# Attention as a side pipeline: two steps per pair of blocks, values together with new scores and both transposes together, let in at half as many places

## The chip, the core and the metric

The kernel runs on one core of a Trainium2 chip. The metric is the device time of one execution in microseconds. The input is one sequence of 512 tokens with 1024 channels, all in float32.

## What is computed

The reference is one layer with two sublayers. The parts that matter here, cut from it:

```python
proj = x @ w_in                                   # q, k, v of 12 heads; zb; qc
# A: three groups of 4 heads, dilations 1, 4, 16, causal windows, 128-query blocks
s = einsum(qb, kb) * ATTN_SCALE + bias            # masked
p = exp(s - s.max(-1)); den = p.sum(-1)
o = einsum(p, vb) / den                           # groups combined by their softmax denominators
# B: gated spatial mixing of gelu(zb).  C: 4 heads of cross-attention into 256 memory tokens
gates = sigmoid(x @ w_gate + b_gate)              # one per branch and channel
merged = gates0 * (oa @ w_proj_a) + gates1 * (ob @ w_proj_b) + gates2 * (oc @ w_proj_c)
h = layer_norm(ALPHA * x + merged @ w_out)
out = layer_norm(ALPHA * h + conv_ffn(h))         # gated MLP with a causal width-3 convolution
```

## The kernel before

Every large product is done in three matmuls (`mm3`, line 220): each operand is split into a high part in the float32r form and the rest, and high x rest, rest x high and high x high are added in PSUM. ScalarE makes the high part of a weight (line 133), VectorE the rest (line 134). Weights stream in on SP's queue, two loads ahead, and are split two units ahead of their use. TensorE does the main work in this order: q and k, v, the two halves of zb (`zb_part`, called twice), mem transposed (`tm`), qc, kc and vc, 24 gate columns (`gate`, with the branch projections between them), the output projection, and the gated MLP.

Attention is side work. It is written as a Python generator, `side()`, and each call of `fill()` in the main work lets one step of it in, up to the next `yield`. First come the windowed heads (`attn_A`) and their combination, which fall into the zb, qc, kc and vc stages; then, from the flag `mix` on, the spatial gating and the cross-attention (`attn_C`), which fall into the gate stage. `fill()` stands after each of 16 row blocks in each half of zb, at some places of qc, kc and vc, and after every second k of the gates.

A `Pair` is two query blocks of one head. An item of the pipeline is two such pairs, of two neighbouring heads, with four pieces of work:
- scores (`sc`, matmuls at line 524). A head has 64 channels, so its matmul uses 64 rows of the array, and the two heads in turn use the two halves of the rows (`alternate`). For the undilated heads and for the cross-attention a block has three matmuls (`mm3_ops`); for the dilated heads it has two in plain float32, which the trace shows as two instructions each.
- softmax on VectorE (bias and maximum, line 475) and ScalarE (exp, line 480), then the division on VectorE.
- transposes (`pt`, line 493): the full array, four or three matmuls of 128 columns per pair, and a copy by ScalarE from PSUM to `pT` (lines 495 to 498).
- values (`oT`, also line 524): the output has 64 rows, so the heads use the two halves of the array's columns.

In the pipeline before, an item takes four steps: scores of item i; the transposes of the first head of item i-1; those of its second head; the values of item i-2. The windowed attention has 8 items, the cross-attention 4. The `sc`, `pt` and `oT` tiles share eight PSUM banks with the main work's accumulators, of which zb holds four.

The text of the kernel is not the order of the engines. The framework's scheduler takes the instructions in the order of the text and moves them by its own model of when each can start; the engines then run that fixed order, each strictly in its own sequence. Table loads of ScalarE, which it needs to change between exp, log and gelu/tanh, are put in afterwards, wherever the order asks for one.

Of the kernel before, what the change touches and what calls it, by code (L numbers as in the profile page):

```python
# [47 lines left out]


def bucket_rows():  # L50
    """Per dilation group the bucket (one-hot, rows 0-31) and the mask (row 32) of each diagonal."""
    rows = np.zeros((N_BUCKETS + 1, 3, VW), np.float32)
    for i in range(VW):
        for g in range(3):
            n = 255 - i if g == 0 else 127 - i
            if g == 0:
                ok, dist = 0 <= n <= 128, n
            elif g == 1:
                ok, dist = n >= 0, 4 * n
            else:  # L60
                ok, dist = n >= 0 and n % 4 == 0, 4 * n
            if ok:
                rows[int(bucket_of(np.array([dist]))[0]), g, i] = 1.0
            else:
                rows[N_BUCKETS, g, i] = NEG
    return rows
# [3 lines left out]
def layer_kernel(  # L70
# [10 lines left out]
    small = ctx.enter_context(tc.tile_pool(name="small", bufs=4))  # L81
# [9 lines left out]
    def bank(name):  # L91
        return psum.tile([P, 512], F32, tag="bank", name=name)

    # ---------------------------------------------------------------- weight stream
    loads, prepared = [], {}
    state = {"load": 0, "split": 0}
    units = []

    def add_load(shape, src, parts):
        """One DMA of `shape`; parts: function raw -> list of (hi shape, raw view)."""  # L100
        n = len(loads)
        loads.append((shape, src))
        for f in parts:
            units.append((n, f))
# [48 lines left out]
        add_load([P, 8, 256], src, [lambda r: r[:, :, 0:128], lambda r: r[:, :, 128:256]])  # L153

    def kcols(w, k0, nk, c0, nc_):
        """Rows k0*128.., a [128, nk, nc_] load in units of 1024 per partition."""
        src = w[k0 * P:(k0 + nk) * P, c0:c0 + nc_].rearrange("(k p) c -> p k c", p=P)
        per = 1024 // nc_
        parts = [lambda r, s=s: r[:, s:s + per, :] for s in range(0, nk, per)]
        add_load([P, nk, nc_], src, parts)  # L160
# [36 lines left out]
    LAST = 6  # L197
# [3 lines left out]
    for i in range(0, NF, 2):  # L201
        src_a = wup[:, i * P:i * P + 256].rearrange("(k p) c -> p k c", p=P)
        src_b = wup[:, D_FF + i * P:D_FF + i * P + 256].rearrange("(k p) c -> p k c", p=P)
        n = len(loads)
# [7 lines left out]
        krows(wdn, k, k < NF - LAST)  # L212

    def mm3_ops(ps, w, v, first, last):
        """ps += w.T @ v for operands split into (hi, lo)."""
        return ((ps, w[1], v[0], first, False), (ps, w[0], v[1], False, False), (ps, w[0], v[0], False, last))

    def mm3(*args):
# [7 lines left out]
        else:  # L226
            nc.vector.scalar_tensor_tensor(lo, src, scale, hi.bitcast(F32), op0=ALU.mult, op1=ALU.subtract)

    # ---------------------------------------------------------------- x, transposed and split
    xraw = []  # L230
    for h in range(2):
        xraw.append(T8(f"x{h}").rearrange("p (b a) c -> p b (a c)", b=2))
# [35 lines left out]
        v = [t[k // 4][:, k % 4, :].rearrange("p (l r) -> p r l", r=4)[:, r, :] for t in (xTh, xTl)]  # L268
        return v[0], v[1]

    # ---------------------------------------------------------------- small parameters
    rows = const.tile([P, P], F32, name="rows")
    nc.vector.memset(rows, 0.0)
    nc.gpsimd.dma_start(rows[0:66, :], conv_w[0].rearrange("c (t p) -> (c t) p", p=P))
# [56 lines left out]
                                    ps.rearrange("p (g q) -> p g q", g=4),  # L331
                                    maskT[:, None, :].to_broadcast([P, 4, P]), op=ALU.mult)

    # ---------------------------------------------------------------- q, k, v
    qk12 = [T8(f"qk{i}") for i in range(2)]
    qk0 = [T8(f"qk0{i}", F32R) for i in range(2)]

# [51 lines left out]
    for j in range(2, 12):  # L389
        w = unit()  # L390
        ps = bank("qk")
# [10 lines left out]
    for hb in range(2):  # L402
        ps = bank("v0")
        for bb in range(2):
            b = 2 * hb + bb
# [13 lines left out]
    for r in range(4):  # L419
        nc.scalar.activation(v12[:, r, :], pss[r], AF.Copy)  # L420

    # ---------------------------------------------------------------- attention pieces
    NM = const.tile([P, 48], F32, name="NM")
    DEN = const.tile([P, 48], F32, name="DEN")
    RD = const.tile([P, 48], F32, name="RD")

    class Pair:
        """Two query blocks of one head: scores, softmax, weighted values (transposed)."""

        def __init__(self, part, h, pr):  # L430
            self.part, self.h, self.pr = part, h, pr
# [3 lines left out]
            return P if self.part == 0 and self.pr == 0 and u == 0 else 0  # L435

        def score_ops(self):
            """Matmul arguments of the scores, in order."""
            part, h, pr = self.part, self.h, self.pr
            rp = slice((h % 2) * HD, (h % 2) * HD + HD)  # L440
            sc = bank("sc").rearrange("p (u c) -> p u c", u=2)
            self.sc = sc
            ops = []
            for u in range(2):
                b = 2 * pr + u
                bs = slice(b * P, (b + 1) * P)
                if part == 1:
                    for g in range(2):
                        j = 2 * (g + 1) + h // 2
                        ops.append((sc[:, u, g * P:(g + 1) * P], qkT(j)[rp, bs], qkT(6 + j)[rp, bs], True, True))  # L450
                elif part == 0:
                    lo = self.lo(u)
                    ops.extend(mm3_ops(sc[:, u, lo:256], [t[rp, bs] for t in qk0s(h // 2)],
                                       [t[rp, (b - 1) * P + lo:(b + 1) * P] for t in qk0s(6 + h // 2)], True, True))
                else:
                    ops.extend(mm3_ops(sc[:, u, :], [t[rp, h // 2, bs] for t in qcT],
                                       [t[rp, h // 2, :] for t in kcT], True, True))
            return ops
# [59 lines left out]
            return ops  # L518

    def alternate(a, b):  # L520
        """The matmuls of two heads in turn: they use different rows or columns of the array."""
        for pair in zip(a, b):
            for ps, w, v, first, last in pair:
                nc.tensor.matmul(ps, w, v, start=first, stop=last)  # L524

    def pipeline(groups):
        """groups: (part, first head, done); scores run two steps ahead of values."""
        items = [[Pair(part, h + i, pr) for i in range(2)] + [gi] for gi, (part, h, _) in enumerate(groups)
                 for pr in range(2)]
        dsts = {}  # L530
        n = len(items)
        for i in range(n + 2):
            if i < n:
                two = items[i][:2]
                alternate(*[it.score_ops() for it in two])
                for it in two:
                    it.softmax()
                yield
            if 0 <= i - 1 < n:
                for it in items[i - 1][:2]:  # L540
                    it.turn()
                    yield
            if i >= 2:
                a, b, gi = items[i - 2]
                if gi not in dsts:
                    dsts[gi] = bank("oT")
                alternate(a.value_ops(dsts[gi]), b.value_ops(dsts[gi]))
                if a.pr == 1:
                    groups[gi][2](dsts[gi])
                yield  # L550

    oA = T8("oA")
# [68 lines left out]
    def fill(n=1):  # L621
        for _ in range(n):
            next(gen, None)
# [2 lines left out]
        while flag not in ready:  # L626
            next(gen)

    # ---------------------------------------------------------------- gated spatial inputs, memory
    sgb = T8("sgb")  # L630
    nc.sync.dma_start(sgb[:, 0, :], sg_ln_g[0:1, :].to_broadcast([P, SG_W]))
    nc.sync.dma_start(sgb[:, 1, :], sg_ln_b[0:1, :].to_broadcast([P, SG_W]))
# [1 line left out]
    def zb_part(dst):  # L634
        pss = [bank(f"zb{b}") for b in range(NB)]
        for u in range(4):
            w = unit()
            for b in range(NB):
                for k2 in range(2):
                    k = 2 * u + k2  # L640
                    xh, xl = xs(k, slice(b * P, (b + 1) * P))
                    mm3(pss[b], (xh, xl), (w[0][:, k2, :], w[1][:, k2, :]), k == 0, k == KD - 1)
                fill()
        for b in range(NB):
            nc.scalar.activation(dst[:, b, :], pss[b], AF.Gelu_apprx_tanh)

# [56 lines left out]
    for b in range(2):  # L703
        for k in range(KD):
            w = ws_[k // 4]
            bs = slice(b * P, (b + 1) * P)
            mm3(ps[:, b * 256:b * 256 + 256], (mTh_[:, k, bs], mTl_[:, k, bs]),
                (w[0][:, k % 4, :], w[1][:, k % 4, :]), k == 0, k == KD - 1)
            if k % 4 == 3:
                fill()  # L710
    nc.vector.tensor_copy(vcN, ps.rearrange("p (b c) -> p b c", b=2))
    ready.add("mix")

    # ---------------------------------------------------------------- spatial gating, cross-attention
    obT_h = T8("obTh", F32R)
    obT_l = T8("obTl", F32R)
    ocT = T8("ocT", F32R)
# [28 lines left out]
        groups = [(2, 2 * hp, evac_C(hp)) for hp in range(2)]  # L746
        yield from pipeline(groups)

    # ---------------------------------------------------------------- gates and branch projections
    m = [T8(f"m{i}") for i in range(2)]  # L750
    mTh = [T8(f"mTh{i}", F32R) for i in range(2)]
    mTl = [T8(f"mTl{i}", F32R) for i in range(2)]
# [27 lines left out]
    for br, (nk, per, src) in enumerate(branches):  # L780
        for f in range(KD):
# [3 lines left out]
            ps = bank("gate")  # L785
            for k in range(KD):
                mm3(ps, (w[0][:, k, :], w[1][:, k, :]), xs(k), k == 0, k == KD - 1)
                if k % 2 == 1:
                    fill()
            t = W2("gt")  # L790
            nc.scalar.activation(t, ps, AF.Tanh, bias=gb5[:, br * 8 + f:br * 8 + f + 1], scale=0.5)
# [2 lines left out]
            late = (br, f, t, wp)  # L794
    merge(*late)

    # ---------------------------------------------------------------- output projection, first norm
    def last_rows(n):
        """Split rows of the last LAST steps of a [*, 1024] weight, kept whole."""
        rows = []  # L800
        for k2 in range(LAST // 2):
            while state["load"] <= n + k2:
# [11 lines left out]
        return hx[b // 2][:, b % 2, :]  # L814

    def project(nk, src, n, norm_in):
        """src (transposed, split) times the weight of the stream; norm_in(b) after each row block."""
        py = [[bank(f"y{b}{hf}") for hf in range(2)] for b in range(NB)]

        def step(b, hf, k, w):  # L820
# [60 lines left out]

    project(KD, lambda k: (M(mTh, k), M(mTl, k)), n_wout, norm1)

    # ---------------------------------------------------------------- gated MLP
    h2 = [T8(f"h2_{i}", F32R) for i in range(NF // 2)]

    def H2(i):
# [32 lines left out]
        up_mm(pb, wb, slice(0, S))  # L920
        up_end(i, pa, pb)

    # ---------------------------------------------------------------- down projection, second norm
    lnp2 = T8("ln2").rearrange("p (k a) c -> p k (a c)", k=2)
    nc.sync.dma_start(lnp2[:, 0, :], ln2_g[0:1, :].to_broadcast([P, D]))
    nc.sync.dma_start(lnp2[:, 1, :], ln2_b[0:1, :].to_broadcast([P, D]))
# [23 lines left out]
```

## Time and profile before

| | |
|---|---|
| time, median of 3 runs | 822.31 us (822.22 to 822.71) |
| span of the profiled execution | 820.5 us |
| TensorE matmuls | busy 807.0 us (98%), 4051 instructions |
| VectorE | busy 382.5 us (47%) |
| ScalarE | busy 284.4 us (35%), 9 table loads |
| score, transpose and value matmuls of attention | 117 to 185 us (windowed), 232 to 272 us (cross) |

The chain of work that ended last runs over TensorE for 98% of the span. Matmuls overlap in the profile: a 512-column one is shown with 0.39 us but the next one starts 0.23 us later. So the busy share says little, and the distance between starts is what a matmul costs.

### The profile page before, as it was taken

The numbers are of one execution on the slowest core, as the hardware profiler recorded it, in microseconds if no ns is written. First come the engines' busy times: TensorE is split into PE (matmuls) and PEld (weight loads), VectorE is DVE, ScalarE is ACT, GpSimd is POOL, SyncE is SP. The second block draws the span as 40 slices with busy tenths as digits, with TensorE's granted clock in tenths as the row PEclk, the third lists the DMA queues.
The fourth block names the chain that finished last, engine by engine and source line by source line (L and its number), as shares of the span: only waits on it lengthen the run. The fifth ranks groups of instructions, "written<-read, shape, count | busy, mean of one in ns | idle before, by whom it ended". The sixth has DMA issues, their size and how long they took to land.

```text
span 820.5 us, 9700 instructions
## 1 busy us (share of the span) xinstructions
PE 807.0 (98%) x4051; PEld 675.0 (82%) x4051; DVE 382.5 (47%) x591; ACT 284.4 (35%) x433; POOL 20.4 (2%) x32
## 2 busy tenths in 40 slices
PE   7999999999999999999999999999999999999996
PEld 6878997778877788888888988888888888888884
DVE  4333235836664334335856455544454445225055
ACT  4331246665365222223611243333333333224000
POOL 2001000100000000000000000000000000000000
PEclk9999999999999999999999999999999999999998
DMA  9355331122402133242840023233333324224002
GB/s 317 124 196 182 103 129 52 52 78 82 150 26 78 52 103 128 78 152 89 323 154 1 1 103 102 103 103 103 103 103 102 103 83 131 94 102 154 1 26 77
DMA packets 62411, 87.10 MB, mean 106 GB/s; under 512 B 1994, under 2 KB 50154, under 8 KB 62368
## 3 DMA queue, kind: packets, MB, share of 16 engines
q1 hardware_dynamic: 60960, 82.32, 29.5%
q0 software_dynamic: 1408, 4.17, 1.5%
q8 instruction: 32, 0.52, 0.3%
q14 instruction: 11, 0.09, 0.0%
HBM read 84.36 MB, written 4.47 MB: 108 GB/s over the span
## 4 chain that ended last, share of the span: by engine, by line
PE 98%; DMA 1%; DVE 0%; SPq 0%; issue 0%; DVEq 0%
PE y L220 20%; PE gate L220 16%; PE pa L220 13%; PE pb L220 13%; PE qk L220 7%; PE zb L220 6%; PE proj L220 5%; PE v L220 4%; PE up L220 3%; PE oT L524 1%; PE sc L524 1%; PE qc L220 1%; PE pt L493 1%; PE qk L362 1%; PE vc L220 1%; PE kc L220 1%
## 5 line engine op out<-in xcount | busy, mean ns | idle before, releaser
L134 DVE TENSOR_TENSOR wl<-raw,wh 128x1024 fp32r<-128x1024 f32 (+1 forms) x127 | 154.1, 1214 | 186.5 <-ACT wh L133 177.7
L133 ACT ACTIVATE wh<-raw 128x1024 fp32r<-128x1024 f32 (+1 forms) x127 | 133.2, 1050 | 192.9 <-PE pb L220 47.2
L220 PE MATMUL y<-wh,h 128*128 128x512 f32 x256 | 79.0, 389 | 0.0
L220 PE MATMUL gate<-xTh,wl 128*128 128x512 f32 x192 | 76.7, 400 | 0.0
L220 PE MATMUL gate<-xTh,wh 128*128 128x512 f32 x192 | 75.0, 390 | 0.0
L220 PE MATMUL gate<-xTl,wh 128*128 128x512 f32 x192 | 74.9, 390 | 0.0
L220 PE MATMUL pa<-hTh,wl 128*128 128x512 f32 x160 | 62.3, 389 | 0.0
L220 PE MATMUL pa<-hTl,wh 128*128 128x512 f32 x160 | 62.3, 389 | 0.0
L220 PE MATMUL pa<-hTh,wh 128*128 128x512 f32 x160 | 62.2, 389 | 0.0
L220 PE MATMUL pb<-hTh,wl 128*128 128x512 f32 x160 | 62.2, 389 | 0.0
L220 PE MATMUL pb<-hTl,wh 128*128 128x512 f32 x160 | 62.2, 389 | 0.0
L220 PE MATMUL pb<-hTh,wh 128*128 128x512 f32 x160 | 62.2, 389 | 0.0
L220 PEld LDWEIGHTS y<-wh,h 128*128 128x128 f32 x256 | 48.0, 188 | 10.1
L220 PE MATMUL y<-wl,h 128*128 128x512 f32 x128 | 49.8, 389 | 0.0
L898 DVE SCALAR_TENSOR_TENSOR c<-pa,par,c 128x511 f32<-128x511 f32 x20 | 15.0, 750 | 65.8 <-ACT c L897 65.8
L220 PEld LDWEIGHTS gate<-xTh,wl 128*128 128x128 f32 x192 | 36.1, 188 | 8.6 <-issue 1.2
L220 PEld LDWEIGHTS gate<-xTh,wh 128*128 128x128 f32 x192 | 36.0, 188 | 7.8
L897 ACT ACTIVATE c<-pa,par 128x512 f32<-128x512 f32 x20 | 15.6, 781 | 76.1 <-PE pa L220 76.1
L220 PEld LDWEIGHTS gate<-xTl,wh 128*128 128x128 f32 x192 | 36.1, 188 | 7.0
L220 PE MATMUL qk<-xTh,wl 128*128 128x512 f32 (+1 forms) x96 | 35.8, 374 | 0.0
L220 PE MATMUL qk<-xTh,wh 128*128 128x512 f32 (+1 forms) x96 | 35.7, 371 | 0.0
L220 PE MATMUL qk<-xTl,wh 128*128 128x512 f32 (+1 forms) x96 | 35.6, 372 | 0.0
(219 smaller groups left out, 1480.8 us busy)
## 6 DMA issues: line engine op xcount, KB each, us to landing
raw<-in_w_ffn_up SPq DMA_DIRECT2D x22, 1024.0 KB, 4.9
raw<-in_w_in SPq DMA_DIRECT2D x13, 1024.0 KB, 5.0
raw<-in_w_gate SPq DMA_DIRECT2D x12, 1024.0 KB, 5.0
raw<-in_w_ffn_down SPq DMA_DIRECT2D x11, 1024.0 KB, 4.7
raw<-in_w_out SPq DMA_DIRECT2D x4, 1024.0 KB, 4.7
shear<-vecs POOLq DMA_DIRECT2D x1, 2304.0 KB, 14.1
raw<-in_w_mem_kv SPq DMA_DIRECT2D x2, 1024.0 KB, 5.3
raw<-in_w_proj_b SPq DMA_DIRECT2D x4, 512.0 KB, 3.3
```

Of the source, the lines that this page charges most:

```text
L133: nc.scalar.activation(h3, src, AF.Copy)
L134: nc.vector.tensor_tensor(l3, src, h3.bitcast(F32), op=ALU.subtract)
L220: nc.tensor.matmul(ps, w, v, start=first, stop=last)
L362: nc.tensor.matmul(ps[:, sl], w[a][:, k, :], xs(k0 + k, sl)[c], start=k0 + i + k == 0, stop=k0 > 0 and i == 2 and k == 3)
L493: nc.tensor.transpose(pt[:, kb, u, :], self.p[:, u, kb * P:(kb + 1) * P], ident)
L524: nc.tensor.matmul(ps, w, v, start=first, stop=last)
L897: nc.scalar.activation(c, pa, AF.Identity, bias=CB(i), scale=CW(2, i))
L898: nc.vector.scalar_tensor_tensor(c[:, 1:], pa[:, :S - 1], CW(1, i), c[:, 1:], op0=ALU.mult, op1=ALU.add)
```

## The change

An item now takes two steps. One holds the values of item i-2 and, behind them, the scores of item i; the other holds the transposes of both heads of item i-1. The calls of `fill()` are halved in zb (after every second row block), vc (once per block instead of twice) and the gates (every fourth k instead of every second); qc and kc keep theirs. Removed docstrings and comment lines are left out of the diff.

```diff
 def pipeline(groups):
         for i in range(n + 2):
-            if i < n:
-                two = items[i][:2]
-                alternate(*[it.score_ops() for it in two])
-                for it in two:
-                    it.softmax()
-                yield
-            if 0 <= i - 1 < n:
-                for it in items[i - 1][:2]:
-                    it.turn()
-                    yield
             if i >= 2:
                 a, b, gi = items[i - 2]
                 if gi not in dsts:
...
                 alternate(a.value_ops(dsts[gi]), b.value_ops(dsts[gi]))
                 if a.pr == 1:
                     groups[gi][2](dsts[gi])
+            if i < n:
+                two = items[i][:2]
+                alternate(*[it.score_ops() for it in two])
+                for it in two:
+                    it.softmax()
+            yield
+            if 0 <= i - 1 < n:
+                for it in items[i - 1][:2]:
+                    it.turn()
                 yield
...
 def zb_part(dst):
-                fill()
+                if b % 2 == 1:
+                    fill()
...
 # vc
-            if k % 4 == 3:
+            if k == 7:
                 fill()
...
 # gates
-                if k % 2 == 1:
+                if k % 4 == 3:
                     fill()
```

The order that the build makes of it differs on TensorE and on ScalarE. Three places follow.

TensorE, the scores of the last pair of blocks of an undilated item, in the second half of zb. A row is one matmul, out<-in, and the number in a tile's name tells tiles of one kind apart: `sc_1282` is one head's scores, `sc_1283` the other's. Before (the two heads go on in turn for 12 rows):

```order
L220 MATMUL zb0_1266<-wl23_1070,xTh0_102 128x512
L220 MATMUL zb0_1266<-wh23_1069,xTh0_102 128x512
L524 MATMUL sc_1282<-qk01_126,qk00_125 128x256
L524 MATMUL sc_1283<-qk01_126,qk00_125 128x256
L524 MATMUL sc_1282<-qk01_126,qk00_125 128x256
L524 MATMUL sc_1283<-qk01_126,qk00_125 128x256
```

The same scores now:

```order
L524 MATMUL sc_1309<-qk01_126,qk00_125 128x256 x6
L220 MATMUL zb0_1252<-wl24_1135,xTh0_102 128x512
L220 MATMUL zb0_1252<-wh24_1134,xTh0_102 128x512
L524 MATMUL oT_1176<-pT_1275,v12_642 64x128
L524 MATMUL oT_1176<-pT_1282,v12_642 64x128
L524 MATMUL oT_1176<-pT_1275,v12_642 64x128
L524 MATMUL oT_1176<-pT_1282,v12_642 64x128
L524 MATMUL oT_1176<-pT_1275,v12_642 64x128
L524 MATMUL oT_1176<-pT_1282,v12_642 64x128
L524 MATMUL oT_1176<-pT_1275,v12_642 64x128
L524 MATMUL oT_1176<-pT_1282,v12_642 64x128
L524 MATMUL sc_1310<-qk01_126,qk00_125 128x256 x6
```

The six scores of one head stand ahead of the values of an older item, and the six of the other head behind them.

ScalarE, from the last exps of the windowed attention to the gelus of the second half of zb. Before:

```order
L480 ACTIVATE p_1458,DEN_878<-p_1458,NM_877 128x256 x2
L498 ACTIVATE pT_1473<-pt_1472 128x512
L567 ACT_TABLE_LOAD
L567 ACTIVATE lse_1622<-DEN_878 128x32
L133 ACTIVATE wh29_1606<-raw16_1432 128x1024
L498 ACTIVATE pT_1486<-pt_1485 128x512
L560 ACTIVATE oA_880<-oT_1421 128x512
L645 ACT_TABLE_LOAD
L645 ACTIVATE ug_1265<-zb0_1266 128x512
L498 ACTIVATE pT_1518<-pt_1517 128x512
L645 ACTIVATE ug_1265<-zb1_1267 128x512
L498 ACTIVATE pT_1531<-pt_1530 128x512
```

Now:

```order
L480 ACTIVATE p_1485,DEN_878<-p_1485,NM_877 128x256
L645 ACT_TABLE_LOAD
L645 ACTIVATE ug_1251<-zb0_1252 128x512
L480 ACT_TABLE_LOAD
L480 ACTIVATE p_1485,DEN_878<-p_1485,NM_877 128x256
L566 ACT_TABLE_LOAD
L566 ACTIVATE lse_1653<-DEN_878 128x32
L559 ACTIVATE oA_880<-oT_1381 128x512
L645 ACT_TABLE_LOAD
L645 ACTIVATE ug_1251<-zb1_1253 128x512
L498 ACTIVATE pT_1510<-pt_1509 128x512
L498 ACTIVATE pT_1517<-pt_1516 128x512
```

One gelu now stands between the two exps of a head, and four table loads stand ahead of the two copies where two stood ahead of the copies before.

TensorE at the end of the second half of zb, up to mem's transposes (`tm`) and qc. Before:

```order
L220 MATMUL zb_1268<-wh_1353,xTh_103 128x512
L524 MATMUL oT<-pT,v_642 64x128 x8
L220 MATMUL zb_1269<-wh_1353,xTl_105 128x512
L220 MATMUL zb_1269<-wl_1354,xTh_103 128x512
L220 MATMUL zb_1269<-wh_1353,xTh_103 128x512
L220 MATMUL zb_1269<-wh_1353,xTl_105 128x512
L220 MATMUL zb_1269<-wl_1354,xTh_103 128x512
L220 MATMUL zb_1269<-wh_1353,xTh_103 128x512
L524 MATMUL oT<-pT,v_642 64x128 x8
L677 MATMUL tm<-ident,memraw 128x128 x16
```

Now:

```order
L220 MATMUL zb_1255<-wh_1339,xTl_105 128x512
L220 MATMUL zb_1255<-wl_1340,xTh_103 128x512
L220 MATMUL zb_1255<-wh_1339,xTh_103 128x512
L524 MATMUL oT<-pT,v_642 64x128 x8
L677 MATMUL tm<-ident,memraw 128x128 x16
L220 MATMUL qc<-xTh_102,wl_1415 128x512
```

The eight values ahead of mem's transposes now read the two copies `pT_1510` and `pT_1517` of the ScalarE rows above; the last values of the windowed attention have moved behind qc's first matmuls.

## Rows read from the trace of the kernel before

**Rows 1.** The page: span, and busy time of each engine.

```profile
span 820.5 us, 9700 instructions
PE 807.0 (98%) x4051; PEld 675.0 (82%) x4051; DVE 382.5 (47%) x591; ACT 284.4 (35%) x433; POOL 20.4 (2%) x32
```

**Rows 2.** Waits of TensorE, whole span: waiter <- releaser: us, times, longest.

```profile
PE tx L259 <- DMA x<-in_x: 5.7, 2, 3.6
```

**Rows 3.** Timeline of TensorE, one visit of scores: start us, us, instruction, count.

```profile
159.85 0.39 PE L220 MATMUL zb<-wl,xTh 128*128 128x512 f32 x1
160.08 0.39 PE L220 MATMUL zb<-wh,xTh 128*128 128x512 f32 x1
160.39 1.16 PE L524 MATMUL sc<-qk,qk 64*128 64x128 f32 x16
161.49 0.50 PE L220 MATMUL zb<-wh,xTl 128*128 128x512 f32 x1
161.82 0.39 PE L220 MATMUL zb<-wl,xTh 128*128 128x512 f32 x1
```

**Rows 4.** Timeline of TensorE, two visits of values, of 12 and of 16 instructions.

```profile
132.45 0.88 PE L524 MATMUL oT<-pT,v 128*64 128x128 f32 x12
133.26 0.50 PE L220 MATMUL zb<-wh,xTl 128*128 128x512 f32 x1
...
149.24 1.09 PE L524 MATMUL oT<-pT,v 128*64 128x128 f32 x16
150.26 0.50 PE L220 MATMUL zb<-wh,xTl 128*128 128x512 f32 x1
150.60 0.39 PE L220 MATMUL zb<-wl,xTh 128*128 128x512 f32 x1
```

**Rows 5.** All transposes as a group (busy us, mean ns); then one visit with values.

```profile
L493 PE MATMUL pt<-ident,p 128*128 128x128 f32 x92 | 14.3, 272 | 0.0
...
139.94 0.60 PE L493 MATMUL pt<-ident,p 128*128 128x128 f32 x4
140.47 1.09 PE L524 MATMUL oT<-pT,v 128*64 128x128 f32 x16
```

**Rows 6.** Timeline of TensorE, scores of 256 columns in the gate stage.

```profile
232.73 0.97 PE L524 MATMUL sc<-kcT,qcT 64*128 64x256 f32 x12
233.63 0.50 PE L220 MATMUL gate<-xTh,wl 128*128 128x512 f32 x1
```

**Rows 7.** Timeline of TensorE near the start, 256-column matmuls on the full array.

```profile
10.28 1.05 PE L362 MATMUL qk<-xTl,wh 128*128 128x256 f32 x4
11.14 0.41 PE L362 MATMUL qk<-xTh,wl 128*128 128x256 f32 x1
...
14.19 0.28 PE L220 MATMUL qk<-xTh,wl 128*128 128x256 f32 x1
14.31 0.28 PE L220 MATMUL qk<-xTl,wh 128*128 128x256 f32 x1
```

**Rows 8.** Timeline of ScalarE at the end of the windowed attention.

```profile
170.85 0.51 ACT L480 ACTIVATE p<-p,NM 128x256 f32<-128x256 f32 x1 [2.77 <-DVE NM L475]
...
171.36 0.49 ACT L480 ACTIVATE p<-p,NM 128x256 f32<-128x256 f32 x1
...
174.73 0.23 ACT L567 ACTIVATE lse<-DEN 128x32 f32<-128x32 f32 x1
...
176.62 0.60 ACT L560 ACTIVATE oA<-oT 128x512 f32<-128x512 f32 x1
177.24 1.28 ACT L645 ACT_TABLE_LOAD   x1
178.53 0.60 ACT L645 ACTIVATE ug<-zb 128x512 f32<-128x512 f32 x1
179.03 0.59 ACT L498 ACTIVATE pT<-pt 128x512 f32<-128x512 f32 x1
```

**Rows 9.** Timeline of VectorE, the step between those scores and their first exp.

```profile
170.32 0.42 DVE L475 CUSTOM_DVE_ANT_0 p<-sc,bias 128x256 f32<-128x256 f32 x1 [0.98 <-PE sc L524]
```

## The prediction

> **What bounds the kernel now.** I read the page first [rows 1]: TensorE is busy for 807.0 of the 820.5 us of the span. A busy TensorE may still be waiting between overlapping matmuls, so next come its waits [rows 2]. The only entry in the whole span is 5.7 us for x at the very start. In the attention stretch no score, transpose or value matmul waits for ScalarE or VectorE. Last I read TensorE's own order in time, because with no waits the time is the sum of the distances between starts. Here the reader is to see three things. A 512-column matmul of the main work takes 0.23 us to the next. A visit to the side work costs more than its matmuls. And VectorE and ScalarE, busy 47% and 35%, cover their parts of the side work completely. So the change can gain only by making TensorE's own order cheaper, and it loses whatever new wait it puts into it.
>
> **What a visit costs.** The 16 score instructions of one pair of heads sit between matmul starts at 160.08 and 161.82 [rows 3], 1.74 us; less two ordinary steps of 0.23 that is 1.28. The body I get from values: 16 of them run from 149.24 to the next matmul in 1.02 us, 12 of them from 132.45 in 0.81 [rows 4], so two couples (both heads side by side) cost 0.21, one couple 0.105. Eight couples are 0.84; the other 0.44 is fixed. For values alone it is (1.02 + 0.34 - 0.23 + about 0.09 at the entry) - 0.84 = 0.38. I take **0.42 us fixed per run of scores or values**. About 0.20 of it are longer steps of the 512-column matmuls around it (0.31 and 0.33 in place of 0.23 in [rows 3]); the rest is the first and last step inside the run. Transposes cost no such thing: four take 0.53 us up to the values behind them [rows 5], 0.11 each plus that run's entry.
>
> **What the order of the change really is.** The diff promises whole joint steps. The built order, quoted in the section on the change, differs: where a step now puts values and scores behind one another, the scheduler has pulled several apart. I count runs of scores or values on TensorE. Before: 16 in the windowed attention and 8 in the cross-attention, 24, none beside another. After: 22 and 9, 31, of which 11 follow a run of the other kind with nothing between.
> - Seven more runs: 7 x 0.42 = **+2.9 us**.
> - Eleven joins. The trace has none. A join loses the two longer 512-column steps, 0.20, and keeps the change of form, as the transposes show: values behind transposes start 0.20 after the last one (139.94 + 3 x 0.11 = 140.27 to 140.47, [rows 5]) where the next transpose would have started after 0.11 (0.60 for four less one matmul of 0.27, over three steps). So -0.20 each, **-2.2 us**; bounds 0 and the whole 0.42, that is 0 to -4.6. I take the value nearest to the transposes' row. The Trainium skill (TensorEngine Tiling (Array Packing), Key Properties) says that changing the tiling mode drains TensorE, tile changes within a mode do not; going from 64-row scores to 64-column values is such a change, so by it a join cannot save the whole 0.42, and the 0.20 step behind the transposes agrees.
> - Heads that no longer run side by side. Twice the scores of one head (6 matmuls of 256 columns) stand alone, and the other head's six behind them: 12 steps in place of 6. A 256-column step on its own is 0.12 (14.19 to 14.31, [rows 7]); six couples took no more, 0.90 with entry and exit [rows 6]. +6 x 0.12 = 0.7. One visit of the four-matmul scores is likewise one head, then the other: +8 x 0.105 = 0.8. Three times one head's single value matmul, two instructions, is cut off from its group: 3 x 0.21 = 0.6. Two more groups of scores are cut: 0.2 each. Together **+2.6 us** (bounds 0, if a lone head cost only half a couple, to +5.4, below).
> - Both heads' transposes in one step: eight at 0.11 cost what two times four cost, -0.1 (0 to -0.3).
>
> TensorE's own work: 2.9 - 2.2 + 2.6 - 0.1 = **+3.2 us**. It lies on the path in full, since nothing else ends later.
>
> **New waits.** ScalarE copies the transposed weights out of PSUM before the values, and runs strictly in its order. At the end of the second zb part that order now is, behind the scores of the last pair: exp, table load, gelu, table load, exp, table load, log, copy of oA, table load, gelu, and only then the two copies that TensorE's next values need. Before, two loads stood there, and values stood behind copies made earlier. Prices [rows 8]: exp 0.51 to the next, load 1.29 (177.24 to 178.53), gelu 0.60 in front of a load and 0.50 otherwise, log 0.23, copy of oA 0.60, copies 0.50 and 0.59. Sum: 0.51 + 1.29 + 0.60 + 1.29 + 0.51 + 1.29 + 0.23 + 0.60 + 1.29 + 0.50 + 0.50 + 0.59 = 9.2 us. The first exp starts some 0.6 us after TensorE has left the scores: VectorE's part runs at 170.32 [rows 9], exp at 170.85. So both copies are there 9.8 us after. In between TensorE has 21 matmuls of 512 columns (4.8), one run of 14 value instructions (8 steps, 0.84 + 0.42 = 1.3) and 8 transposes (0.9): 7.0 us. TensorE waits 9.8 - 7.0 = **2.8 us**, at the values in front of the transposes of mem; queued behind them are those transposes and all matmuls of qc, and everything later waits with them. No later slack takes it back, because TensorE waits for nothing afterwards [rows 2].
>
> The same happens in small at the end of the first zb part: copy of oA 0.60, load 1.29, two gelus 1.0, the copy 0.59, that is 3.5 us behind a run of values, against 8 transposes and 10 matmuls, 3.2 us: **0.4 us** with the latency of the semaphores (0 to 0.8). SP's weight loads and POOL's few instructions keep their order; the weight splits on ScalarE move by a visit at most and are made two units ahead of their use, so I cost them at nothing. The merged steps halve how often the side work is let in, but a step is twice as large, so the stages end where they did, well before their users.
>
> **Sum.** +3.2 of work and +3.2 of waits: the profiled execution goes from 820.5 to 826.9 us of span. The median of the three runs is 822.31, 1.8 us above that span for what lies around it; with the same 1.8 the time is **828.7 us**.
>
> **Rivals.**
> - Joins are worth the whole fixed cost: 11 x 0.22 less, 826.3 us. For it: a run's entry and exit look alike in the rows. Against: the 0.20 behind transposes.
> - ScalarE is in time, both waits are hidden: 825.5. For it: the trace has no such wait now. Against: four loads in a row are 5.2 us on an engine that does nothing else meanwhile.
> - The wait lowers TensorE's clock. At the start, after idling, 256-column matmuls stand 0.21 us apart (10.28 to 11.14 for four), the lower level of 1.2 GHz; from 14.19 on 0.12, the upper one of 2.4 GHz [rows 7]. The same 3.9 us at the lower level cost about half of it: 830.7. Against: the wait is shorter than the idling at the start. [...]
> - Weight loads of one head come in series, because no other head fills the gap: a step that cannot overlap takes 0.20 in place of 0.105 [rows 5], 28 lone steps x 0.10 = 2.8, 831.5. [...] The 0.12 steps of the full array [rows 7], each with new weights in the same rows, disagree.
> - The other side: TensorE runs the steps as the source reads, not as the printed order says. Place: all visits that are cut in the order. Then there are 24 runs, 8 joins at 0.20 to 0.42 (-1.6 to -3.4), no lone heads and copies in time: 820.7 to 818.9, middle 819.8, faster. It decides if no run of one head's six scores stands alone in the trace. Against: the printed order of before is met in its trace (the transposes in front of values in [rows 5] stand so).
> - No waits and free joins together: 823.1, no change.
>
> **How the numbers follow.** Forecast 55%, joins free 11%, waits hidden 11%, clock 9%, serial weight loads 6%, as the source reads 5%, both savings at once 3%. The predicted time is the forecast's. The range runs from 825.0, below hidden waits, to 831.6, just over serial loads; it leaves out the 8% of the last two and the outer tails. Faster and slower count from 0.2%, 1.6 us, about what a measurement of this kernel can tell from no change: faster 5%, same 5% (the 3% and the lower edge of hidden waits), slower 90%.
>
> **What would show it.** In the profile of the changed kernel TensorE's waits should list values (oT) behind the copies pT, one of 2 to 3 us just ahead of the transposes of mem, and four table loads on ScalarE within some 7 us before it. A lone run of six scores should take about 0.7 us to its last step, and scores straight behind values should start 0.2 us after them. I am wrong if no such wait is listed, if joined runs follow at 0.1 us, or if the time is below 825.

## The result, and the profile after

| | before | after |
|---|---|---|
| time, median of 5 runs | 822.41 us (822.22 to 822.71) | 829.04 us (827.64 to 829.59) |
| span of the profiled execution | 820.5 us | 827.6 us |
| TensorE busy | 807.0 us | 811.0 us |

The ratio is 1.008 (95% interval 1.0069 to 1.009): the change makes the kernel slower, and the time is 0.3 us from the predicted 828.7. How much of that agreement is earned comes out below.

First the page of the changed kernel, answering to [rows 1]: the span, and each engine's busy time.

```profile
span 827.6 us, 9698 instructions
PE 811.0 (98%) x4051; PEld 678.7 (82%) x4051; DVE 383.1 (46%) x591; ACT 283.8 (34%) x433; POOL 19.9 (2%) x32
```

TensorE has the same 4051 matmuls and 4 us more, in a span that is 7 us longer. Its waits, answering to [rows 2] (waiter <- releaser: us, times, longest):

```profile
PE tx L259 <- DMA x<-in_x: 6.0, 2, 3.9
PE oT L524 <- ACT pT L498: 2.5, 2, 2.3
PE qk L220 <- DVE wl L134: 0.2, 1, 0.2
```

The second line is new: values wait for the copies that ScalarE makes of the transposed weights. (The third lies at the start of the kernel, ahead of the attention.) To see where the 7 us are, I cut the span at two matmuls that both kernels have: the last of v, just ahead of the attention, and the first of the output projection, just behind the gates. These are the stretches between their starts, in the kernel before and in the changed one (us, then busy us and count by engine, and PEclk, the granted clock):

```profile
115.33:405.17 289.84, 289.84 (x1583) 235.64 (x1582) 149.84 (x297) 131.85 (x244) 3.77 (x4) 1.00 0.30 101
```

```profile
115.00:412.21 297.21, 294.61 (x1582) 240.49 (x1582) 150.42 (x297) 131.33 (x244) 3.31 (x4) 0.99 0.29 98
```

The stretch is 7.37 us longer. The start of the kernel was 0.33 us quicker in this execution (115.33 to 115.00) and the end alike. So this stretch is what has to be explained. Its clock is 0.99: for a while it was not full. Here is TensorE at the place where the long wait is (start us, us, instruction, count):

```profile
184.56 0.39 PE L220 MATMUL zb<-wh,xTh 128*128 128x512 f32 x1
187.25 1.72 PE L524 MATMUL oT<-pT,v 128*64 128x128 f32 x16 [2.30 <-ACT pT L498]
188.90 3.44 PE L677 MATMUL tm<-ident,memraw 128*128 128x128 f32 x16
192.09 0.49 PE L220 MATMUL qc<-xTh,wl 128*128 128x512 f32 x1
192.42 0.39 PE L220 MATMUL qc<-xTl,wh 128*128 128x512 f32 x1
```

No matmul starts for 2.69 us, and the 16 transposes of mem behind the wait take 3.19 us, 0.20 each, nearly twice the 0.11 of [rows 5]. The granted clock says why:

```profile
184.56:187.25 2.69, 0.39 (x2) 0.00 (x1) 0.00 (x0) 2.66 (x5) 0.00 (x0) 1.00 0.00 0
188.55:191.96 3.41, 3.41 (x19) 3.10 (x17) 2.26 (x3) 2.46 (x5) 0.00 (x0) 0.50 0.02 1
```

The clock falls to the lower level of 1.2 GHz 1.3 us after the values have begun, stays there for 3.41 us and is full again after that (1.00 from 191.96 to 200.00). And this is ScalarE over the same time, answering to [rows 8]:

```profile
178.34 0.51 ACT L480 ACTIVATE p<-p,NM 128x256 f32<-128x256 f32 x1 [0.34 <-DVE NM L475]
...
178.96 1.28 ACT L645 ACT_TABLE_LOAD   x1
180.26 0.60 ACT L645 ACTIVATE ug<-zb 128x512 f32<-128x512 f32 x1
180.87 1.28 ACT L480 ACT_TABLE_LOAD   x1
182.17 0.51 ACT L480 ACTIVATE p<-p,NM 128x256 f32<-128x256 f32 x1
...
182.79 1.28 ACT L566 ACT_TABLE_LOAD   x1
184.08 0.23 ACT L566 ACTIVATE lse<-DEN 128x32 f32<-128x32 f32 x1
184.22 0.58 ACT L559 ACTIVATE oA<-oT 128x512 f32<-128x512 f32 x1
184.82 1.28 ACT L645 ACT_TABLE_LOAD   x1
186.11 0.60 ACT L645 ACTIVATE ug<-zb 128x512 f32<-128x512 f32 x1
186.61 1.08 ACT L498 ACTIVATE pT<-pt 128x512 f32<-128x512 f32 x2
```

Four table loads stand among the last exps and ahead of the two copies that TensorE waits for; the first copy, 0.59 long, ends at 187.20, and the values start at 187.25.

The small wait stands ahead of the values at the end of the first zb part. They start 0.63 us after the last main matmul, where such an entry takes 0.31 to 0.32 without a wait (160.08 to 160.39 in [rows 3]), so it costs 0.31:

```profile
146.97 0.39 PE L220 MATMUL zb<-wh,xTh 128*128 128x512 f32 x1
147.60 0.43 PE L524 MATMUL oT<-pT,v 128*64 128x128 f32 x2 [0.24 <-ACT pT L498]
```

### The profile page after: what moved, and what is told of

Its sections match the earlier page's. It is cut to its first block, busy times and chain, and to the rows that moved or that the text cites. A ratio compares the mean times of both kernels' runs of the same rounds, so it can differ in the third digit from the quotient of the medians.

```text
span 827.6 us, 9698 instructions
## 1 busy us (share of the span) xinstructions
PE 811.0 (98%) x4051; PEld 678.7 (82%) x4051; DVE 383.1 (46%) x591; ACT 283.8 (34%) x433; POOL 19.9 (2%) x32
## 4 chain that ended last, share of the span: by engine, by line
PE 96%; ACT 1%; DMA 1%; DVE 1%; issue 0%; SPq 0%; DVEq 0%; ACTq 0%
PE y L220 20%; PE gate L220 16%; PE pa L220 13%; PE pb L220 13%; PE qk L220 7%; PE proj L220 5%; PE zb L220 5%; PE v L220 4%; PE up L220 3%; PE sc L524 2%; PE oT L524 1%; PE qc L220 1%; PE pt L493 1%; DMA raw<-in_w_in 1%; PE vc L220 1%; PE kc L220 1%
```

## The experiments

The theory to be tested has three parts: the joint steps that the scheduler cut up are the added work, the table loads on ScalarE are the wait, and the wait lowers the clock. The runs move them singly and together. Only one execution of each kernel has a profile. For the others the sign of a lower clock is the mean granted clock of the execution, and it is not a sharp one: every profile also ends with 2.6 to 5.3 us at the lower level, when TensorE's work is done, and the kernel before, whose profile shows no other fall, shows means of 0.996 to 0.999. In the changed kernel it is 0.995 in four of the five runs and 0.997 in the quickest. Where "by the stretch" is said below, it is the profiled time from the last matmul of v to the first of the output projection, against the 289.84 us of the kernel before.

**The log later.** One load and the log leave the chain; TensorE's order is that of the changed kernel. `keep_in_program_order` puts an instruction behind what the source has issued on its engine so far.

```diff
-        nc.scalar.activation(lse, DEN[:, 0:32], AF.Ln)
+        tc.keep_in_program_order(nc.scalar.activation(lse, DEN[:, 0:32], AF.Ln))
```

> TensorE's order is that of the changed kernel; only the log of the combination, with the table load that it needs, moves behind the four gelus of the second zb part. My theory (the long wait is ScalarE's chain of table loads): one load of 1.29 us and the log of 0.23 fall out of the chain ahead of the two copies, so the wait at the values ahead of mem's transposes shrinks by 1.5 us from some 2.4 to 0.9 and the time from 829.0 to 827.5; if the lower clock after it was caused by the wait and a shorter one does not bring it, 1.7 us more goes, 825.8. Rival (the wait has another cause, for instance VectorE or the PSUM banks): the wait stays at 2.4 us and the time at 829.0.

Measured: 826.54 us (826.42 to 827.44). TensorE at the place:

```profile
184.90 0.39 PE L220 MATMUL zb<-wh,xTh 128*128 128x512 f32 x1
186.04 1.58 PE L524 MATMUL oT<-pT,v 128*64 128x128 f32 x16 [0.76 <-ACT pT L498]
187.55 1.97 PE L677 MATMUL tm<-ident,memraw 128*128 128x128 f32 x16
```

The gap between starts shrinks from 2.69 to 1.14 us, by the 1.5 of one load and a log. The clock does not fall behind it (mean 0.997 or 0.998 in all five runs), and the transposes are shown with 1.97 us in place of 3.44. So the wait is ScalarE's chain, and a shorter one leaves the clock alone.

**Tanh for gelu.** Two loads fewer, without touching the order of TensorE. The kernel leaves out gelu in the second half of zb.

```diff
-            nc.scalar.activation(dst[:, b, :], pss[b], AF.Gelu_apprx_tanh)
+            nc.scalar.activation(dst[:, b, :], pss[b], act)
...
-    zb_part(ug)
+    zb_part(ug, AF.Tanh)
```

> The four gelus of the second zb part are replaced by tanh, so gelu is left out there; tanh needs no other table than exp. TensorE's order is that of the changed kernel, and two of the four loads between the last exps and the two copies fall out. My theory: 2.6 us less stand in front of the copies, the long wait falls from 2.4 us to 0 to 0.3; with it the lower clock behind it goes (1.7 us): 829.0 - 2.4 - 1.7 = 824.9, or 826.6 if the clock falls all the same. Rival (the wait is not made by the loads): 829.0.

Measured: 825.10 us (824.78 to 825.83). TensorE at the place:

```profile
184.86 0.39 PE L220 MATMUL zb<-wh,xTh 128*128 128x512 f32 x1
185.18 1.10 PE L524 MATMUL oT<-pT,v 128*64 128x128 f32 x16
186.21 1.97 PE L677 MATMUL tm<-ident,memraw 128*128 128x128 f32 x16
...
188.24 0.39 PE L220 MATMUL qc<-xTl,wh 128*128 128x512 f32 x1
```

From the last zb matmul to the second of qc it is now 3.38 us, where the changed kernel had 7.86 (184.56 to 192.42). The difference, **4.48 us**, is the price of the long wait: 2.37 until the first copy is there (2.69 less the ordinary 0.32), 1.7 for 3.41 us at half the clock (an estimate, half of its length), and the 0.4 that is left, at the values of the second head, whose copy comes last. By the stretch 292.72 us are left, 2.88 more than before. That is the added work and the small wait, which is still there.

```profile
115.30:408.02 292.72, 292.48 (x1582) 238.85 (x1582) 150.11 (x297) 126.75 (x241) 3.31 (x4) 1.00 0.30 100
```

**Whole joint steps.** From zb to the gates TensorE issues in the order of the source.

```diff
+    def order_pe(ins):
+        if pin["on"]:
+            tc.keep_in_program_order(ins)
...
-            nc.tensor.matmul(ps, w, v, start=first, stop=last)
+            order_pe(nc.tensor.matmul(ps, w, v, start=first, stop=last))
...
-                nc.tensor.matmul(ps, w, v, start=first, stop=last)
+                order_pe(nc.tensor.matmul(ps, w, v, start=first, stop=last))
```

(The transposes and the other matmuls likewise; `pin` is on from the first zb part to the last gate.)

> The change with its joint steps kept whole: from zb to the end of the gates TensorE issues in the order of the source, so every joint step is the values of both heads side by side and straight behind them the scores of both heads side by side. 24 runs of scores or values instead of 31, 8 joins instead of 11, no lone heads; the long wait for ScalarE's chain stays. My theory (the cut-up steps are the work that the change adds): 7 x 0.42 = 2.9 less, 3 x 0.20 = 0.6 more, lone heads 2.6 less, the small wait in the first zb part 0.3 less: 829.0 - 5.2 = 823.8. Rival 1 (cut or whole, the joint step itself is dear): 828 to 829. Rival 2 (the order of the source makes TensorE wait in new places, as the scheduler avoided): 829 or more.

Measured: 823.25 us (822.11 to 824.78, 11 runs); ratio to before 1.0014 (1.0005 to 1.0022). TensorE's order has 24 runs of scores or values and 8 joins, where the changed kernel's has 31 and 11. The long wait is still there, with a gap of 2.40 us, and in the profiled run so is the lower clock, 0.50 from 183.23 to 186.65. Much of the spread goes with the clock: at a mean of 0.997 or 0.998 six runs took 822.1 to 823.3, at 0.995 or 0.996 five took 823.5 to 824.8. The gap, and the stretch:

```profile
179.90 0.39 PE L226 MATMUL zb<-wh,xTh 128*128 128x512 f32 x1
182.30 2.07 PE L530 MATMUL oT<-pT,v 128*64 128x128 f32 x16 [2.02 <-ACT pT L504]
```

```profile
114.93:406.96 292.03, 289.95 (x1583) 237.98 (x1582) 150.29 (x297) 129.84 (x243) 3.48 (x4) 0.99 0.30 100
```

Cutting up the steps was most of the loss: the stretch is 5.18 us shorter than in the changed kernel, with the long wait and the lower clock in both profiles. 0.6 of it is the shorter gap (2.40 for 2.69) and the small wait, which is gone; 4.6 is left for the cuts.

**Whole joint steps and the log later**, both edits together.

> Both edits together: joint steps whole, and the log behind the gelus, so that one table load stands in front of the two copies. My theory: no wait at all is left behind x at the start, so 2.7 us less than the whole steps alone, and the clock does not fall (1.7 us): 823.8 - 4.4 = 819.4; counted from the kernel before, 8 joins x 0.20 = 1.6 and eight merged visits of transposes 0.2 to 0.4 less give 820.5. So 819.4 to 820.5, faster than both kernels. Rival 1 (the clock falls there whatever TensorE does before): 821.1 to 822.2. Rival 2 (joins save nothing, what a trace shows at one join is given back around it): 822.2, no change to the kernel before.

Measured: **820.29 us** (819.83 to 820.48, 7 runs), ratio to before 0.9975 (0.9965 to 0.9986): faster than both kernels. TensorE waits for nothing between 100 and 300 us. The stretch takes 287.85 us, 2.0 less than before:

```profile
115.10:402.95 287.85, 287.85 (x1583) 236.36 (x1583) 150.01 (x297) 128.25 (x242) 3.48 (x4) 1.00 0.30 102
```

**The wait filled.** Matmuls without use where TensorE idles, in the changed kernel.

```diff
+                if gi == 3 and a.pr == 0:
+                    for k in range(11):
+                        tc.keep_in_program_order(nc.tensor.matmul(
+                            dsts[gi], xTh[0][:, 0, 0:P], xTh[0][:, 1, :], start=True, stop=True))
                 alternate(a.value_ops(dsts[gi]), b.value_ops(dsts[gi]))
```

> The changed kernel with 11 more 512-column matmuls on the full array (11 x 0.23 = 2.5 us) put ahead of the values that wait so long; they write the bank that those values then overwrite. Nothing else moves. Theory (TensorE's idling of 2.4 us is what makes its clock fall): the added matmuls run inside the wait and cost nothing, some 0.4 us of the wait for the second copy is left, the granted clock stays full in every run, and the 1.7 us of the low stretch are saved: 829.0 - 1.7 = 827.3. Rival 1 (the clock falls there for another reason, for instance what the other engines do): 829.0, with the low stretch in most runs. Rival 2 (the wait is not idle time, the added matmuls push everything back): 831.5.

Measured: 827.84 us (827.47 to 828.18), by the stretch (115.50 to 411.10) 1.6 us less than the changed kernel, with 2.5 us of matmuls more. TensorE at the place, and the granted clock over the time in which it had fallen:

```profile
185.28 2.65 PE L539 MATMUL oT<-xTh 128*128 128x512 f32 x11
187.87 1.46 PE L524 MATMUL oT<-pT,v 128*64 128x128 f32 x16
```

```profile
188.55:191.96 3.41, 3.41 (x34) 3.10 (x29) 1.81 (x3) 3.41 (x7) 0.00 (x0) 1.00 0.00 0
```

The values start 0.1 us later than in the changed kernel, counted from the last matmul of v, and the clock is full; its mean was 0.997 or 0.998 in all five runs. It was TensorE's idling that lowered it.

**The wait longer**, in the kernel with whole steps.

```diff
+            if self.col == 16 + 8:
+                nc.scalar.activation(t[:, 0, 0, 0:1], pt[:, 0, 0, 0:1], AF.Ln,
+                                     bias=RD[:, self.col:self.col + 1])
```

> The whole joint steps of e3 with one more log, and so one more table load, on ScalarE between the transposes and the two copies that the long wait is for; TensorE's order is that of e3, where the wait of 2.0 us brought the lower clock in 5 of 11 runs (824.0 to 824.8 with it, 822.1 to 823.5 without). Theory (the longer TensorE idles the surer its clock falls, and the fall costs the same 1.7 us each time): the wait grows by load 1.29 + log 0.3, by 1.6 us to some 3.6 to 4.1, and the clock falls in every run: 822.6 + 1.6 + 1.7 = 825.9. Rival 1 (the fall is chance, whatever the length of the wait): about half of the runs near 824.2, the others near 825.9. Rival 2 (a longer wait costs a longer stretch at the lower level, in proportion to the wait): 827 or more, low stretch about 6 us.

Measured: 826.34 us (825.69 to 826.66), with a mean clock of 0.995 in all five runs. The matmuls around the wait, and the low stretch:

```profile
180.85 0.39 PE L226 MATMUL zb<-wh,xTh 128*128 128x512 f32 x1
185.31 1.98 PE L533 MATMUL oT<-pT,v 128*64 128x128 f32 x16 [4.08 <-ACT pT L507]
```

```profile
185.16:188.57 3.41, 3.26 (x23) 2.93 (x24) 0.00 (x0) 3.38 (x6) 0.00 (x0) 0.50 0.01 2
```

The gap is 4.46 us now, the low stretch still 3.41. Rival 2 is out, and so is a chance that is the same at every length: by the mean clock of each run, the lower level came in none of 5 runs behind a gap of 1.14 us, in 4 or 5 of 11 behind 2.40 (four took 824.0 or more; the run of 823.48 has a mean of 0.996, which the kernel before shows too), in 4 of 5 behind 2.69 and in 5 of 5 behind 4.46. That the fall is surer behind 2.69 than behind 2.40 these few runs do not show.

**The old fills.** The halving undone. The scheduler's order on TensorE changes with it, to 36 runs of scores or values and 14 joins.

```diff
-                if b % 2 == 1:
-                    fill()
+                fill()
...
-            if k == 7:
+            if k % 4 == 3:
...
-                if k % 4 == 3:
+                if k % 2 == 1:
```

> One part of the change undone: the side work is let in as often as before (every row block in zb, twice per block in vc, every second k in the gates), the two-step pipeline stays. A pair's transposes then stand 18 main matmuls (4.1 us) and some visits behind its scores, where it was 30 before and is 36 in the change. Theory (the halving is what gives softmax its time: two steps let in at the old rate are too near): waits of several us at transposes and values, two of them long enough to lower the clock: 829.0 - 1.7 - 2.7 + 10 + 2 x 1.7, 834 to 839. Rival (softmax of a pair is short enough, the halving only spreads visits): 826 to 829, with joins as in the change.

Measured: 838.50 us (837.68 to 839.09). TensorE's waits:

```profile
PE pt L493 <- DVE p L485: 5.3, 2, 4.7
PE oT L524 <- ACT pT L498: 2.6, 1, 2.6
```

and the clock, behind the first wait and behind the second:

```profile
158.25:165.08 6.83, 6.25 (x35) 4.78 (x36) 4.08 (x18) 2.56 (x10) 0.00 (x0) 0.50 0.01 4
...
171.90:175.32 3.42, 3.33 (x8) 2.33 (x9) 0.76 (x3) 0.52 (x2) 0.00 (x0) 0.50 0.00 0
```

In the order that the scheduler makes, two steps per pair do not work at the old rate: the transposes come before the softmax is done. Whether they would with the joint steps kept whole was not run.

**The transposes alone.** The kernel before with both heads' transposes in one step.

```diff
                 for it in items[i - 1][:2]:
                     it.turn()
-                    yield
+                yield
```

> The other part alone: the kernel before with both heads' transposes in one step, nothing else (steps of scores and of values apart, side work let in as before). Theory (transposes have almost no fixed cost: four cost 0.45, eight 0.88 of a visit): 12 merged visits save at most 0.2, with some more or less from where the scheduler puts things: 821.7 to 822.2, no change. Rival 1 (a visit of transposes has a fixed cost like one of scores, 0.2 to 0.4): 12 x 0.3 less, 818.6. Rival 2 (with both heads' copies behind one another on ScalarE the values come too late): 823 or more, with waits at oT.

Measured: 821.79 us (821.40 to 822.33, 11 runs), ratio 0.9996 (0.9987 to 1.0005): no change. TensorE's order has 25 runs here and two joins, so it holds one more cut beside the merged transposes.

## Why the prediction was right, point by point

The mechanisms were the right ones: more runs on TensorE, and a wait for table loads. That the number agrees to 0.3 us is partly luck, because errors in its terms cancel. Against the kernel before, the profiled stretch shows:

| term | predicted | measured |
|---|---|---|
| TensorE's own work | +3.2 | +2.6 (2.88 less the small wait of 0.31) |
| long wait | +2.8 | +2.8 (2.37 + 0.41) |
| small wait | +0.4 | +0.3 |
| clock | 0 (a rival, +2.0 on top) | +1.7, in 4 of 5 runs |
| start of the kernel | 0 | -0.3 |

- **Long wait.** Place, cause and size hold. The chain was put at 9.2 us from its exp to the last copy; it took 9.35 (178.34 to 187.69). A load cost 1.30 to the next start each time (178.96 to 180.26). The Trainium skill (ScalarE: Activation LUTs, What ACT_TABLE_LOAD costs) adds a drain to every switch and comes to about 2.66 us; the rows here show none: a load starts 0.01 to 0.11 us behind the end of the instruction shown before it, and the next one starts 0.01 to 0.02 behind the load.
- **Joins.** Predicted -0.20 each, and that is what they bring. Twelve values with 16 scores straight behind them:

```profile
131.16 0.39 PE L220 MATMUL zb<-wh,xTl 128*128 128x512 f32 x1
131.48 0.88 PE L524 MATMUL oT<-pT,v 128*64 128x128 f32 x12
132.29 1.16 PE L524 MATMUL sc<-qk,qk 64*128 64x128 f32 x16
133.38 0.50 PE L220 MATMUL zb<-wl,xTh 128*128 128x512 f32 x1
133.72 0.39 PE L220 MATMUL zb<-wh,xTh 128*128 128x512 f32 x1
```

  The values take 0.81 up to the scores, as they took 0.81 up to the next main matmul in [rows 4]: the change of form is paid all the same, and only the longer main steps of one visit fall away. Start to start 2.56 us, less two steps of 0.23, is 2.10; the two visits apart are 1.02 ([rows 4] with an entry of 0.32) and 1.28 ([rows 3]). The rival of free joins is out. That agrees with the page on tiling (the Trainium skill, TensorEngine Tiling (Array Packing), Key Properties), by which a new mode always drains.
- **Lone heads.** A lone head's six scores cost as much as both heads' twelve, as predicted:

```profile
156.88 0.97 PE L524 MATMUL sc<-qk,qk 64*128 64x256 f32 x6
157.77 0.50 PE L220 MATMUL zb<-wl,xTh 128*128 128x512 f32 x1
...
158.44 1.09 PE L524 MATMUL oT<-pT,v 128*64 128x128 f32 x16
159.46 0.97 PE L524 MATMUL sc<-qk,qk 64*128 64x256 f32 x6
160.37 0.50 PE L220 MATMUL zb<-wh,xTl 128*128 128x512 f32 x1
```

  Six take 0.89 and 0.91 us to the next main matmul, twelve took 0.90 [rows 6]. Neither half the price nor serial weight loads (0.20 a step) fit.
- **The sum of the work** is 0.6 too high. The runs split it in two: whole steps without the long wait are 2.0 below the kernel before, where I had eight joins and the merged transposes at 1.7; the cuts then cost 2.57 + 2.0 = 4.6, where I had 4.9 (seven runs at 0.42, three joins fewer to pay it back, 2.6 for lone heads). Adding up the visits in the traces (each from the main matmul before it to the second behind it, less two ordinary steps) gives 48.2 us before, 51.3 in the run with tanh and 46.2 with whole steps and the log later. So visits add 2.8 beside the small wait: the cuts cost 4.7 and whole steps save 1.9. Another 0.25 is saved outside all visits, in the main matmuls, and no term of the sum stood for that. No price in the sum is far off. The dearest cut, eight scores, one head's single value and eight scores more, takes 2.53 us from 175.24 to the next main matmul at 177.77, where the scores in [rows 3] take 1.10: 1.43 more, charged with 1.49 (two runs less two joins, 0.44, and 1.05 for lone heads).
- **The clock** is the step that failed. I gave the rival of a lower clock 9%, since the wait was shorter than the idling at the start. It came in four of five runs, behind a gap of 2.69 us, and it came again behind one of 2.40. So the length of the wait beside that of the idling at the start was no argument against it. The median of 829.04 has the fall in it; the one run whose mean clock was 0.997, like those of the kernel before, took 827.64. Without the fall the forecast would have been 1.1 us too high; with it, the surplus in the work, the small wait and the quicker start (of one execution against one other) made up for 1.0 of the 1.7. That is the luck in the number.
- **The other side**, that TensorE runs as the source reads, was priced at 819.8. The time of that order is now measured: 820.29 with the waits away. What TensorE ran in the changed kernel was the printed order, as the lone runs of six scores above show.

## What to carry to other kernels

Merging steps of a source does not merge them on the engine: the scheduler issued the cut order, and forcing the order of the source gave back 5 us. Before a merge is costed, the built order of the bounding engine and of the engine that feeds it should be read, and the table loads in front of each copy that TensorE needs counted. A wait of TensorE can cost more than its length: behind the gaps of 2.40 and 2.69 us here some executions lost 1.7 us more to the lower clock.

## What had not been expected of the hardware

The lower clock did not come with the gap that brought it: in the changed kernel it began 1.3 us after the first matmul behind the gap, with whole steps 0.9 after it, with the longer wait 0.15 us ahead of it. It lasted 3.41 us whether the gap was 2.40, 2.69 or 4.46 us (6.83 once, with the old fills). For gaps of 2.40 and 2.69 us it came in some executions of the same program and not in others, so that two runs of one kernel can differ by some 1.7 us (half of 3.41, an estimate); what decides it in a given run these experiments leave open.
